# Forgetting heads' norms from whole squares, and the second four heads' keys turned by DMA

## The chip, the cores and the metric

The kernel runs on one core of one Trainium2 chip. The metric is the device time of one execution in microseconds (us); a lower time is better. PE is TensorE, ACT is ScalarE, DVE is VectorE, POOL is GpSimd and SP is SyncE, which issues most of the DMAs. PEld is the weight load of PE.

## The reference, cut to what matters

One layer on 256 tokens of width 2048: a combined projection, two groups of attention heads side by side, an output projection, and a feed-forward part. The change touches the queries and keys of the forgetting group, which has 8 heads of 128 columns:

```python
def rms_norm(x, g):
    x32 = x.astype(jnp.float32)
    y = x32 * lax.rsqrt(jnp.mean(x32 * x32, axis=-1, keepdims=True) + EPS)
    return (y * g.astype(jnp.float32)).astype(x.dtype)
...
    qa = rms_norm(to_heads(qa, N_HEADS_FOX), q_norm_l)
    ka = rms_norm(to_heads(ka, N_HEADS_FOX), k_norm_l)
    log_f = jax.nn.log_sigmoid((fa + b_forget_l).astype(jnp.float32))
    c = jnp.cumsum(log_f, axis=1).transpose(0, 2, 1)
    out_a = forgetting_attention(qa, ka, to_heads(va, N_HEADS_FOX), c)
```

So each head's row of 128 numbers is divided by the root of its mean square, and then queries and keys are needed with the head's columns on the partitions, which takes a transpose.

## The kernel before

All products are float32 split in two parts: ACT casts a weight block `w_raw` to its high part `w_hi` (line 277), DVE subtracts to get the low part `w_lo` (line 285), and PE multiplies with both. A *step* is one weight block. The code hands each step's instructions to the engines in a fixed order that is written out by hand (a schedule without a planner): in the loop at the end, at step n the cast and the subtraction of step n+2 are issued, the load of step n+6, and then the products of step n. Between groups of products `tick()` lets each unfinished piece of side work (a Python generator) run to its next `yield`. So one `yield` more or less moves all that follows in that piece by one tick, about one group of 12 matmuls on PE. Each engine works through its own list strictly in that order.

The projection is done in *units* of 11 steps. Unit A gives the queries and keys of forgetting heads 0 to 3 (tiles `rA00`, `rA01` for queries, tokens 0 to 127 and 128 to 255; `rA10`, `rA11` for keys), unit B those of heads 4 to 7 (`rB..`), unit C queries and keys of four stick-breaking heads (`rC..`), then a unit for values and unit D. Within a unit the products go to four PSUM banks in the order a, c, b, (e, b), a, (e, b), a, b, (c, a), a, (a, c); a pair in brackets is one step with two groups. Between them ACT (line 601) or DVE (line 607) takes a bank's contents out and the bank is then written on. The products of `oFox` and of the heads run beside the next units.

When a unit of the forgetting group is done, `fox_rows(half)` starts: squares and sums of squares of each head, the inverse root (`rsqrt`), the multiplication of the rows by it on DVE (line 710), then the transposes. For heads 0 to 3 the keys are turned by DMA: `send_heads` lets ACT put the two 16-bit halves of each word apart (line 646), SP issues a DMA transpose (line 650), and `take_heads` puts the halves together again (line 655). The queries, and before the change the keys of heads 4 to 7 too, are turned by PE against the identity (line 687, tile `ps_h`) and copied out by ACT (line 691). Then each head runs as `fox_head`: `ps_s` are its scores on PE, `qk` the split queries and keys, `pT` the turned weights, `ps_o` its output, which lands in `oFox`. Until a head lands, its part of `oFox` is not in use.

Of the kernel before, what the change touches and what calls it, by code (L numbers as in the profile page):

```python
# [12 lines left out]
AF = mybir.ActivationFunctionType  # L13
ALU = mybir.AluOpType
AX = mybir.AxisListType
# [4 lines left out]
NT = S // P  # L20
KT = D // P
HD = 128
# [25 lines left out]
def hybrid_layer(  # L48
# [20 lines left out]
    act, dve = nc.scalar, nc.vector  # L69
# [43 lines left out]
    gq = const.tile([P, 1], F32, name="gq")  # L113
# [20 lines left out]
    zeros = ccol.rearrange("p a b -> p (a b)")[:, :P]  # L134
# [32 lines left out]
    def rsqrt(out_, ss, scale, n, gap=2):  # L167
        a = small.tile([P, n], F32, name="rs_a", tag=f"rs_a{n}")
        y = small.tile([P, n], F32, name="rs_y", tag=f"rs_y{n}")
        u = small.tile([P, n], F32, name="rs_u", tag=f"rs_u{n}")  # L170
        dve.tensor_scalar(a, ss, scale, EPS, op0=ALU.mult, op1=ALU.add)
        for _ in range(gap):
            yield
        act.activation(y, a, AF.Ln)
        act.activation(y, y, AF.Exp, scale=-0.5)
        dve.tensor_tensor(u, a, y, op=ALU.mult)
        dve.tensor_tensor(u, u, y, op=ALU.mult)
        dve.tensor_scalar(u, u, -0.5, 1.5, op0=ALU.mult, op1=ALU.add)
        dve.tensor_tensor(out_, y, u, op=ALU.mult)
# [159 lines left out]
    oFox = late.tile([P, NH, S], F32, name="oFox")  # L339
# [11 lines left out]
    def heads_tile(name):  # L351
        return at.tile([P, 4, S], F32, name=name, tag="qk", bufs=2)
# [25 lines left out]
    tile_of = {}  # L378
# [264 lines left out]
    def send_turned(rows, room, moves=(act.copy, dve.tensor_copy)):  # L643
        planes = room.bitcast(U16).rearrange("p h s -> p (h s)").rearrange("p (t c) -> p t c", t=NT)
        for t, (move, (source, words)) in enumerate(zip(moves, rows)):
            move(
                planes[:, t].rearrange("p (b f) -> p b f", b=2),
                source.bitcast(U16).rearrange("p (f b) -> p b f", b=2),
            )
            nc.sync.dma_start_transpose(  # L650
                words.bitcast(U16).rearrange("p (g s) -> p g s", s=P), planes[:, t]
            )

    def take_turned(move, words, t, room):
        move(
            room.bitcast(U16).rearrange("p h (s b) -> p b h s", b=2)[:, :, :, t * P : (t + 1) * P],
            words.bitcast(U16).rearrange("p (b h s) -> p b h s", b=2, h=4),
        )

    def send_heads(rows, n, key, moves=(act.copy, dve.tensor_copy)):  # L660
        tile_of[key] = heads_tile(key)
        send_turned([(rows[n, t], rows[n, t]) for t in range(NT)], tile_of[key], moves)

    def take_heads(rows, n, key, moves):
        for t, move in enumerate(moves):
            take_turned(move, rows[n, t], t, tile_of[key])
# [13 lines left out]
    def to_heads(rows, which, keys, scales):  # L680
        for n, key, scale in zip(which, keys, scales):
            dst = tile_of[key] = heads_tile(key)
            pss = []
            for t in range(NT):
                ps = psb.tile([P, 4, P], F32, name="ps_h", tag="t")
                for h in range(4):
                    nc.tensor.transpose(ps[:, h, :], rows[n, t][:, h * HD : (h + 1) * HD], ident)
                pss.append(ps)
            yield
            for t in range(NT):  # L690
                act.activation(dst[:, :, t * P : (t + 1) * P], pss[t], AF.Identity, scale=scale)

    def fox_rows(half):
        def done(rows):
            order = [(1, 0), (1, 1), (0, 1), (0, 0)]
            ss = small.tile([P, 4, 4], F32, name="ss", tag="ss")
            rn = small.tile([P, 4, 4], F32, name="rn", tag="rn")
            for m, nt in enumerate(order):
                for h in range(4):
                    act.activation(  # L700
                        zeros, rows[nt][:, h * HD : (h + 1) * HD], AF.Square,
                        accum_out=ss[:, m, h : h + 1],
                    )
                if m < 3:
                    yield
            flat = "p a b -> p (a b)"
            yield from rsqrt(rn.rearrange(flat), ss.rearrange(flat), 1.0 / HD, 16)
            for m, nt in enumerate(order):
                r3 = rows[nt].rearrange("p (h d) -> p h d", h=4)
                dve.tensor_tensor(r3, r3, rn[:, m, :].unsqueeze(2).to_broadcast([P, 4, HD]), op=ALU.mult)  # L710
                if m % 2:
                    yield
                    if m == 1 and not half:
                        send_heads(rows, 1, "kA0", (act.copy, act.copy))
            while started["fox"] < 4 * half:
                yield
            if half:
                yield from to_heads(rows, (1, 0), ("kA1", "qA1"), (1.0, gq))
            else:
                yield  # L720
                yield from to_heads(rows, (0,), ("qA0",), (gq,))
                take_heads(rows, 1, "kA0", (act.copy, dve.tensor_copy))
            for h in range(4 * half, 4 * half + 4):
                waiting.append(fox_head(h, half))

        return done
# [808 lines left out]
```

## Time and profile before

| | us |
|---|---|
| median of 3 runs | 1088.14 (1087.89 to 1088.5) |
| the profiled execution's own time | 1089.65 |
| its span in the trace | 1087.9 |
| PE busy | 1082.6 |
| DVE busy | 929.5 |
| ACT busy | 776.1 |

The span is what the trace covers from the first instruction to the last. PE's busy time says that there is nearly always a matmul under way, and that is the first thing to hold against any change here: work taken off PE counts in full, and any new gap on PE counts in full as well. The page's other parts (waits, chain, stretches of the timeline) tell where PE was near a gap.

### The profile page before, as it was taken

The page shows a single profiled execution, that of the slowest core. Times are in us where ns is not written, and L with a number is a line of the kernel's source. Part 1 is how long each engine was busy: PE and PEld are TensorE (multiplying, and loading weights), DVE is VectorE, ACT ScalarE, POOL GpSimd, SP SyncE. Part 2 cuts the span into 40 slices and gives each one's busy share as a digit, 9 for nine tenths or more (in the row PEclk, how much of TensorE's full clock was granted, in tenths as well). Part 3 has the DMA queues.
Part 4 walks back from the last instruction along what each step waited for, and adds up shares of the span by engine and source line. Part 5 has one row for each costly group of instructions (what it writes and reads, how often), then busy time and mean ns, then how long its engine had stood idle before and what let it go on. Part 6 is the DMA issues. An engine that isn't in the chain of part 4 may idle for free.

```text
span 1087.9 us, 14614 instructions
## 1 busy us (share of the span) xinstructions
PE 1082.6 (100%) x5635; PEld 932.2 (86%) x5635; DVE 929.5 (85%) x928; ACT 776.1 (71%) x981; POOL 59.0 (5%) x53
## 2 busy tenths in 40 slices
PE   9999999999999999999999999999999999999998
PEld 9988888888878888888888888888888888888887
DVE  5988899898997877779888988889888898879896
ACT  6767798887876857667766767667767766667663
POOL 0000000001000000000000000000000010000000
PEclk9999999999999999999999999999999999999999
DMA  8897988999876666579899597987969698996995
GB/s 311 267 274 234 306 190 241 245 258 290 244 231 222 193 201 195 192 182 263 252 242 300 172 274 250 255 287 178 310 195 294 219 245 261 232 308 168 284 244 156
DMA packets 192688, 262.85 MB, mean 242 GB/s; under 512 B 22105, under 2 KB 115691, under 8 KB 192619
## 3 DMA queue, kind: packets, MB, share of 16 engines
q1 hardware_dynamic: 169162, 214.59, 59.5%
q0 software_dynamic: 23280, 47.19, 24.5%
q8 instruction: 44, 0.72, 0.3%
q14 instruction: 26, 0.20, 0.1%
q10 hardware_dynamic: 176, 0.14, 0.0%
HBM read 255.48 MB, written 2.10 MB: 237 GB/s over the span
## 4 chain that ended last, share of the span: by engine, by line
PE 89%; DVE 5%; issue 2%; DMA 2%; ACT 1%; DVEq 0%; ACTq 0%; POOLq 0%
PE pu L1268 41%; PE bank_a L305 16%; PE bank_b L305 10%; PE bank_c L305 6%; PE acc_o L305 5%; PE acc_v L425 4%; PE bank_e L305 3%; DVE w_lo L285 2%; DMA w_raw<-in_w_down_dram 2%; PE acc L305 2%; ACT w_hi L277 1%; PE ps_x L195 1%; PE ps_o L775 0%; DVE w_raw L996 0%; DVE xb L1290 0%
## 5 line engine op out<-in xcount | busy, mean ns | idle before, releaser
L285 DVE TENSOR_TENSOR w_lo<-w_raw,w_hi 128x2048 fp32r<-128x2048 f32 (+2 forms) x251 | 555.7, 2218 | 120.5 <-ACT w_hi L277 119.6
L277 ACT CAST w_hi<-w_raw 128x2048 fp32r<-128x2048 f32 (+2 forms) x251 | 464.4, 1853 | 205.1 <-PE pu L1268 84.4
L1268 PE MATMUL pu<-hT,w_hi 128*128 128x512 f32 x1408 | 333.5, 389 | 0.0
L1268 PEld LDWEIGHTS pu<-hT,w_hi 128*128 128x128 f32 x1408 | 262.9, 188 | 53.7
L1268 PEld LDWEIGHTS pu<-hT,w_lo 128*128 128x128 f32 x1408 | 180.0, 191 | 6.6
L1268 PE MATMUL pu<-hT,w_lo 128*128 128x256 f32 x1408 | 182.0, 283 | 0.0
L1321 POOL DMA_DIRECT2D w_raw<-in_w_down_dram x31 | 39.8, 1302 | 714.7 <-DVE w_lo L285 383.1
L1193 ACT ACTIVATE tap<-up,ccol 128x256 f32<-128x256 f32 x176 | 74.6, 495 | 0.0
L305 PE MATMUL bank_a<-w_hi,hT 128*128 128x512 f32 x192 | 48.6, 395 | 0.0
L305 PEld LDWEIGHTS bank_a<-w_hi,hT 128*128 128x128 f32 x192 | 35.2, 188 | 6.9
L305 PE MATMUL bank_b<-w_hi,s 128*128 128x512 f32 x160 | 40.1, 392 | 0.2 <-DVE xb L1290 0.2
L305 PE MATMUL bank_a<-w_hi,s 128*128 128x512 f32 x160 | 40.0, 392 | 0.0
L305 PE MATMUL bank_a<-w_hi,g 128*128 128x512 f32 x152 | 38.0, 392 | 0.0
L425 PE MATMUL acc_v<-w_hi,hT 128*128 128x344 f32 x192 | 36.1, 330 | 0.0
L305 PEld LDWEIGHTS bank_b<-w_hi,s 128*128 128x128 f32 x160 | 28.8, 189 | 5.8 <-issue 0.6
L305 PEld LDWEIGHTS bank_a<-w_hi,s 128*128 128x128 f32 x160 | 28.9, 189 | 5.2
L1186 ACT ACTIVATE gate<-up,ccol 128x256 f32<-128x256 f32 x44 | 24.1, 594 | 11.5 <-DVE up L1179 6.2
L1198 DVE TENSOR_TENSOR gate<-gate,tap 128x512 f32<-128x512 f32 x44 | 30.3, 688 | 2.3
L1198 DVE TENSOR_TENSOR val<-val,tap 128x512 f32<-128x512 f32 x44 | 30.3, 688 | 2.3
L305 PE MATMUL acc_o<-w_hi,oSb 128*128 128x512 f32 x128 | 31.7, 396 | 0.0
L1179 DVE TENSOR_TENSOR up<-t,R 128x512 f32<-128x512 f32 x44 | 30.5, 692 | 1.5
L305 PEld LDWEIGHTS bank_a<-w_hi,g 128*128 128x128 f32 x152 | 27.4, 189 | 5.0
(312 smaller groups left out, 1427.4 us busy)
## 6 DMA issues: line engine op xcount, KB each, us to landing
w_raw<-in_w_up_dram SPq DMA_DIRECT2D x88, 1024.0 KB, 6.8
w_raw<-in_w_down_dram SPq DMA_DIRECT2D x44, 1024.0 KB, 7.1
w_raw<-in_w_in_dram SPq DMA_DIRECT2D x40, 1024.0 KB, 6.8
w_raw<-in_w_down_dram POOLq DMA_DIRECT2D x31, 1024.0 KB, 9.9
w_raw<-in_w_out_dram SPq DMA_DIRECT2D x16, 1024.0 KB, 6.2
w_raw<-in_w_in_dram POOLq DMA_DIRECT2D x10, 1024.0 KB, 9.9
w_raw<-in_w_in_dram SPq DMA_DIRECT2D x13, 516.0 KB, 5.3
xb<-in_x_dram POOLq DMA_DIRECT2D x4, 512.0 KB, 9.3
```

The source lines that it names most:

```text
L195: nc.tensor.transpose(ps[:, j, t * P : (t + 1) * P], x2[:, t, (k + j) * P : (k + j + 1) * P], ident)
L277: copy(hi[:, :n], raw[:, :n])
L285: dve.tensor_tensor(lo[:, :n], raw[:, :n], f32(hi[:, :n]), op=ALU.subtract)
L305: nc.tensor.matmul(o, lhs(i, l, t), r[:, i, :] if cut is None else r[:, i, cut], start=starts and j == 0, stop=stops and j == 3 * n - 1, s ...
L425: nc.tensor.matmul(banks[j][t][:, :VC], of_half(hT[:, k], l, t), w[:, 0, m * VC : (m + 1) * VC], start=k == l == 0 and w is mem["parts", i ...
L1179: dve.tensor_tensor(u[:, :, 2:], t2, R, op=ALU.mult)
L1186: act.activation(a[:, j, :], u[:, j, 2:], AF.Identity, scale=ccol[:, 2, f : f + 1], bias=ccol[:, 3, f : f + 1],)
L1193: act.activation(taps[w][:, j, :], u[:, j, w : w + S], AF.Copy, scale=ccol[:, w, f : f + 1])
L1198: dve.tensor_tensor(a, a, tap, op=ALU.add)
L1268: nc.tensor.matmul(acc[:, j, S:] if low else acc[:, j, :], (lo if low else hi)[:, i, j * P : (j + 1) * P], hT[:, k, 0, :] if low else hT[: ...
L1321: nc.gpsimd.dma_start(mem[weights].rearrange("p (a b) -> p a b", a=4), plus, accum_op=ALU.add)
```

## The change

Three things change in `fox_rows`, for both halves unless said otherwise.

1. The 16 squares per half, each of one head's 128 columns with ACT's own sum (`accum_out`), become 4 squares of whole rows of 512 columns without a sum. They are written into `oFox`, and DVE sums the heads with 4 reductions to 4 values per row.
2. Two rows are squared per tick in place of one, so the piece has two `yield`s ahead of `rsqrt` and not three.
3. For heads 4 to 7 (`half` 1) the keys are no longer turned by PE but by DMA, as those of heads 0 to 3 are, with the upper half of `oFox` as the room for the 16-bit halves; ACT does all four of the copies around the two DMA transposes. `to_heads` then turns the queries alone.

```diff
-            for m, nt in enumerate(order):
-                for h in range(4):
-                    act.activation(
-                        zeros, rows[nt][:, h * HD : (h + 1) * HD], AF.Square,
-                        accum_out=ss[:, m, h : h + 1],
+            for first in (0, 2):
+                squared = [oFox[:, 2 * m : 2 * m + 2, :].rearrange("p a s -> p (a s)") for m in (first, first + 1)]
+                for m, rows_squared in enumerate(squared):
+                    act.activation(rows_squared, rows[order[first + m]], AF.Square)
+                yield
+                for m, rows_squared in enumerate(squared):
+                    dve.tensor_reduce(
+                        ss[:, first + m, :], rows_squared.rearrange("p (h d) -> p h d", h=4),
+                        axis=AX.X, op=ALU.add,
                     )
-                if m < 3:
-                    yield
...
-                    if m == 1 and not half:
-                        send_heads(rows, 1, "kA0", (act.copy, act.copy))
+                    if m == 1:
+                        if half:
+                            room = oFox[:, 4:8, :]
+                        else:
+                            room = tile_of["kA0"] = heads_tile("kA0")
+                        send_turned([(rows[1, t], rows[1, t]) for t in range(NT)], room, (act.copy, act.copy))
             while started["fox"] < 4 * half:
                 yield
             if half:
-                yield from to_heads(rows, (1, 0), ("kA1", "qA1"), (1.0, gq))
+                tile_of["kA1"] = heads_tile("kA1")
+                take_heads(rows, 1, "kA1", (act.copy, act.copy))
+                yield from to_heads(rows, (0,), ("qA1",), (gq,))
```

Lines behind the change stand a little lower in the new file: 710 becomes 712, and lines from 719 on move by 8 (the scores of a head from 798 to 806, for instance). The new squares are line 701, the new reductions line 704.

The change also moves instructions. Three places matter. The first is PE in unit C, from the score and output products around head 3 to the first transposes of unit B's rows. Before:

```order
L305 MATMUL bank_e_1463<-w_hi_1458,hT_95 128x512 x8
L305 MATMUL bank_e_1463<-w_lo_1459,hT_95 128x512 x4
L775 MATMUL ps_o_1576<-pT_1512,vA0_714 128x256 x2
L775 MATMUL ps_o_1576<-pT_1512,vA1_715 128x256
L798 MATMUL ps_s_1580<-cR_121,headR_92 128x384
L802 MATMUL ps_s_1580<-qk_1518 128x256 x3
L777 MATMUL ps_o_1576<-turned_1476,vA2_716 128x128
L804 MATMUL ps_s_1580<-kA0_1178,qA0_1216 128x128
L305 MATMUL bank_b_1432<-w_hi_1458,hT_95 128x512 x8
L305 MATMUL bank_b_1432<-w_lo_1459,hT_95 128x512 x4
L687 MATMUL ps_h_1615<-cs_84,rB10_1047 128x128 x4
L687 MATMUL ps_h_1620<-cs_84,rB11_1048 128x128 x4
```

The same place on PE now:

```order
L783 MATMUL ps_o_1541<-pT_1484,vA0_714 128x256 x2
L783 MATMUL ps_o_1541<-pT_1484,vA1_715 128x256
L806 MATMUL ps_s_1545<-cR_121,headR_92 128x384
L810 MATMUL ps_s_1545<-qk_1490 128x256 x3
L785 MATMUL ps_o_1541<-turned_1443,vA2_716 128x128
L812 MATMUL ps_s_1545<-kA0_1151,qA0_1189 128x128
L305 MATMUL bank_e_1470<-w_hi_1465,hT_95 128x512 x8
L305 MATMUL bank_e_1470<-w_lo_1466,hT_95 128x512 x4
L687 MATMUL ps_h_1594<-cs_84,rB00_1043 128x128 x4
L687 MATMUL ps_h_1599<-cs_84,rB01_1044 128x128 x4
L305 MATMUL bank_b_1430<-w_hi_1465,hT_95 128x512 x8
L305 MATMUL bank_b_1430<-w_lo_1466,hT_95 128x512 x4
```

The key transposes (`rB10`, `rB11`) are gone. The query transposes (`rB00`, `rB01`), which stood two groups further down (behind the group of bank a that follows this bank b), now stand between the groups e and b; and the products of head 3 stand one group earlier, ahead of e.

The second place is DVE in the same stretch of unit C, from the subtraction of step 4 on. Before:

```order
L285 TENSOR_TENSOR w_lo_1427<-w_raw_1164,w_hi_1426 128x2048
L819 RECIPROCAL rl_1449<-l_1445 128x2
L820 TENSOR_SCALAR pr_1446<-pr_1446,rl_1449 128x128
L821 TENSOR_SCALAR pr_1446<-pr_1446,rl_1449 128x256
L285 TENSOR_TENSOR w_lo_1459<-w_raw_1319,w_hi_1458 128x2048
L807 TENSOR_TENSOR ps_s_1477<-ps_s_1477,masksR_118 128x2x128
L809 TENSOR_REDUCE nm_1488<-ps_s_1477 128x1
L810 TENSOR_REDUCE nm_1488<-ps_s_1477 128x1
L171 TENSOR_SCALAR rs_a_1495<-ss_1389 128x16
```

The same place on DVE now, up to the subtraction of step 5:

```order
L827 RECIPROCAL rl_1416<-l_1412 128x2
L828 TENSOR_SCALAR pr_1413<-pr_1413,rl_1416 128x128
L829 TENSOR_SCALAR pr_1413<-pr_1413,rl_1416 128x256
L704 TENSOR_REDUCE ss_1386<-oFox_115 128x4 x2
L285 TENSOR_TENSOR w_lo_1425<-w_raw_1163,w_hi_1424 128x2048
L815 TENSOR_TENSOR ps_s_1444<-ps_s_1444,masksR_118 128x2x128
L817 TENSOR_REDUCE nm_1455<-ps_s_1444 128x1
L818 TENSOR_REDUCE nm_1455<-ps_s_1444 128x1
L704 TENSOR_REDUCE ss_1386<-oFox_115 128x4 x2
L171 TENSOR_SCALAR rs_a_1460<-ss_1386 128x16
L285 TENSOR_TENSOR w_lo_1466<-w_raw_1316,w_hi_1465 128x2048
```

Four reductions came in, and the head's work, `rs_a` and all that leads to the scaled rows stand one subtraction earlier than before. Between here and the scaling of the last row, `rB00`, there were the subtractions of steps 4 to 7; now there are those of steps 4 to 6.

The third place is ACT behind `rsqrt`'s logarithm and exponential, in unit C. Before:

```order
L174 ACTIVATE rs_y_1496<-rs_a_1495 128x16
L175 ACTIVATE rs_y_1496<-rs_y_1496 128x16
L601 ACTIVATE rC10_1397<-bank_a_1366,nrstd1_93 128x512
L277 CAST w_hi_1558<-w_raw_1290 128x2048
L860 ACTIVATE oFox_115<-ps_o_1576,pcol_86 128x256
L781 ACTIVATE ssq0_116<-ps_o_1576 128x256
L838 COPY turned_1515<-pr_1446 128x2x384
L851 CAST pT_1608<-turned_1515 128x256
L831 COPY turned_1611<-pr_1542 128x768
L277 CAST w_hi_1625<-w_raw_1430 128x2048
```

The same place on ACT now:

```order
L277 CAST w_hi_1523<-w_raw_1228 128x2048
L646 COPY oFox_115<-rB10_1045 128x1024
L646 COPY oFox_115<-rB11_1046 128x1024
L601 ACTIVATE rC10_1392<-bank_a_1368,nrstd1_93 128x512
L277 CAST w_hi_1563<-w_raw_1292 128x2048
L868 ACTIVATE oFox_115<-ps_o_1541,pcol_86 128x256
L789 ACTIVATE ssq0_116<-ps_o_1541 128x256
L846 COPY turned_1487<-pr_1413 128x2x384
L859 CAST pT_1584<-turned_1487 128x256
L839 COPY turned_1587<-pr_1508 128x768
L655 COPY kA1_1590<-rB10_1045 128x2x4x128
L655 COPY kA1_1590<-rB11_1046 128x2x4x128
```

The cast of step 8's weights (`w_hi_1625` before, `w_hi_1626` now), which stood directly behind line 831, now comes behind the two copies of line 655, head 3's two exponentials (lines 824 and 825) and the two evictions of the queries (line 691).

On SP the two new DMA transposes stand behind the load of unit C's last block and ahead of the load of the next unit's first.

## Prediction

> **What bounds the kernel now.** I read the page's parts 1 and 4 first, then PE's waits, then the chain, stretches and single rows around the two places where `fox_rows` runs.
>
> ```profile
> PE 1082.6 (100%) x5635; PEld 932.2 (86%) x5635; DVE 929.5 (85%) x928; ACT 776.1 (71%) x981; POOL 59.0 (5%) x53
> PE 89%; DVE 5%; issue 2%; DMA 2%; ACT 1%; DVEq 0%; ACTq 0%; POOLq 0%
> PEld acc_o L305 <- DVE xb L1104: 1.3, 3, 0.5
> PEld bank_b L305 <- ACT rB L601: 0.4, 1, 0.4
> ```
>
> PE bounds it: it is busy for 1082.6 of 1087.9 us, and its longest waits are near 1 us. So work off PE counts once, and a new gap counts once. The question is whether PE's operands still come in time where the change moves them, and the busy shares of the whole span don't tell that. The stretches do (us from the start; then length, busy us of PE, PEld, DVE, ACT, POOL):
>
> ```profile
> 98.00:114.00 16.00, 16.00 (x70) 12.83 (x70) 13.12 (x8) 15.13 (x41) 1.28 (x1) 1.00 0.92 222
> 139.00:157.00 18.00, 18.00 (x87) 15.03 (x86) 16.79 (x23) 17.62 (x51) 1.28 (x1) 1.00 0.84 197
> 157.00:172.00 15.00, 15.00 (x80) 12.67 (x79) 13.92 (x27) 14.81 (x26) 0.00 (x0) 1.00 0.99 282
> 172.00:188.00 16.00, 16.00 (x79) 13.55 (x78) 15.51 (x18) 13.90 (x22) 1.28 (x1) 1.00 0.75 216
> ```
>
> Around half 0 (first row) DVE has 2.9 us to spare in 16. Around half 1 (second and third) it has 2.3 in 33, and ACT 0.6. PE doesn't wait there all the same, because weights are split two steps ahead. This is PE's side of half 1, from the chain (start, length, what):
>
> ```profile
> 158.25 2.72 PE bank_e L305 x12
> 160.97 0.35 PE ps_o L775 x3
> 161.32 0.18 PE ps_s L798
> 161.50 0.35 PE ps_s L802 x3
> 161.85 0.22 PE ps_o L777 x2
> 162.07 0.22 PE ps_s L804 x2
> 162.29 2.76 PE bank_b L305 x12
> 165.05 0.87 PE ps_h L687 x8
> 165.93 2.81 PE bank_a L305 x12
> 168.73 0.87 PE ps_h L687 x8
> 169.61 2.79 PE bank_b L305 x12
> 172.40 0.36 PE ps_o L775 x3
> 172.76 0.22 PE ps_o L777 x2
> 172.98 2.74 PE bank_c L305 x12
> ```
>
> **What PE gains.** The key transposes at 165.05 go: 0.87 us. The wait of 0.4 us on ACT's line 601 stood behind a group of four squares; in half 0 ACT now reaches that eviction earlier, so I count half of it, 0.2 us. Together -1.1 us. These are the only terms on the path that must fall.
>
> **The squares on ACT and DVE.**
>
> ```profile
> L700 ACT ACTIVATE ccol<-rB x16: 302/312/324, 140.9 to 155.0; 128x128 f32<-128x128 f32 x16
> L700 ACT ACTIVATION_READ_ACCUMULATOR ccol<-rB x16: 185/187/207, 141.1 to 155.2; 128x1 f32 x16
> L213 ACT ACTIVATE spare<-xb x8: 616/632/635, 357.0 to 382.5; 128x512 f32<-128x512 f32 x8
> L810 DVE TENSOR_REDUCE nm<-ps_s 128x1 f32<-128x256 f32 x3 | 1.2, 413 | 0.0
> L809 DVE TENSOR_REDUCE nm<-ps_s 128x1 f32<-128x128 f32 x2 | 0.6, 292 | 0.1
> ```
>
> ACT loses 16 x (0.31 + 0.19 less some overlap, 0.43 from start to start) = 7 us per half and gets 4 x 0.63 = 2.5 us. This gain of 4.5 us is off PE's path. DVE gets 4 reductions over 512 columns. No row shows one; from 128 to 256 columns the reduction grows by 0.12 us, so 512 give 0.41 + 0.24 = 0.65 us, about 0.57 from start to start. Bounds are 0.41 (the row with 256) and 0.75 (line 607 on 512). That is 2.3 us more per half for DVE, the engine with 2.3 us to spare, between 1.6 and 3.0. In half 0 the spare 2.9 us and a tick's distance cover it.
>
> **The step that decides: the last row's scaling against PE's query transposes.** PE now wants `rB00` between the groups e and b: 160.97 (end of e) + 1.32 (head 3's five small groups, now ahead of e), less 0.1 to 0.2 for the earlier gain: 162.2. DVE's list ends with the scaling of `rB00`:
>
> ```profile
> 147.13 2.28 DVE L285 TENSOR_TENSOR w_lo<-w_raw,w_hi 128x2048 fp32r<-128x2048 f32 x1
> L285 DVE TENSOR_TENSOR w_lo<-w_raw,w_hi 128x2048 fp32r<-128x2048 f32 x5 | 11.4, 2285 | 1.9 <-ACT w_hi L277 1.9
> L793 DVE TENSOR_TENSOR qk<-kA,qk 128x256 fp32r<-128x256 f32 x2 | 0.8, 418 | 0.0
> 167.03 1.28 DVE L710 TENSOR_TENSOR rB<-rB,rn 128x512 f32<-128x512 f32 x2
> ```
>
> The second and third rows are of the stretch from 147.1 to 168.4. Before, from step 3's subtraction at 147.13 to the scaled `rB00` at 168.31 lie 21.2 us. Of them go: the idle 1.9 (DVE now has the reductions to do while the casts finish), one subtraction 2.2 (step 7's, now behind), and head 2's `qk` pair 0.55, which now stands ahead. The reductions add 2.3. That makes 18.9 us. Step 3's subtraction starts at about 147.2, as before: between the subtractions of steps 1 and 3 stand the same pieces, with head 2's `qk` pair in place of head 1's, which has moved ahead in turn. So `rB00` is ready at 166.1. PE waits 3.9 us for it. Once PE goes on, it is behind before's order by 166.1 - 162.3 = 3.8, and by 3.8 - 0.87 = 2.9 after the second set of transposes that it no longer has. With reductions at 0.41 this is 2.1; at 0.75, 3.4. Beforehand, at 158.1, head 3's `qk` and head 0's `pT` on DVE are late by some 0.4 us; that lies inside the same wait.
>
> **The wait behind it.** ACT's first copy of line 646 needs `rB10` scaled. Counted the same way this is done 5.0 us before `rB00` (`rB11` 0.6, step 6's subtraction 2.2, head 3's mask and maxima 1.0, two rows 1.2), at 161.1. ACT stood at this place at 159.9 before (162.32 below, less a cast and an eviction), and with fewer squares ahead it is now there at about 158. So ACT stands still for 3 us, and what is queued behind is: an eviction of bank a (needed by PE only two groups on), the cast for step 7, head 0's output, and then the two copies of line 655 ahead of the cast for step 8.
>
> ```profile
> L646 ACT COPY kA<-rA x2: 1043/1045/1047, 116.7 to 117.7; 128x1024 uint16<-128x1024 uint16 x2
> L655 ACT COPY kB<-rD x2: 1364/1368/1372, 298.7 to 299.9; 128x1024 uint16<-128x1024 uint16 x2
> 162.32 0.47 ACT L860 ACTIVATE oFox<-ps_o,pcol 128x256 f32<-128x256 f32 x1
> 165.10 1.91 ACT L277 CAST w_hi<-w_raw 128x2048 fp32r<-128x2048 f32 x1
> 174.28 0.74 DVE L607 SCALAR_TENSOR_TENSOR rC<-bank_a,nrstd,rC 128x512 f32<-128x512 f32 x1
> L650 SPq DMA_TRANSPOSE rA<-kA x2: 1607/2484/3361, 117.8 to 119.5; - x2
> rA<-kA SPq DMA_TRANSPOSE x2, 5.4
> rD<-kB SPq DMA_TRANSPOSE x2, 7.2
> ```
>
> From 161.1: two copies 2.0, the eviction 0.6, a cast 1.8, five pieces of heads 2.8 (162.32 to 165.10), two copies 2.7, head 3's exponentials 0.9, two evictions of queries 1.2, the cast of step 8 1.9: 175.0, where that cast ended at 167.0 before. The DMA transposes, issued near 162.3 and 164.0, land by 169.4 at 5.4 us, just before the second copy wants the second of them (169.6); at 7.2 they add 1.5 us. Then DVE: step 8's subtraction 2.2, an addition 0.7, head 4's `qk` 0.6, step 9's subtraction 2.2, the addition out of bank a (line 607, at 174.28 before) 0.7: 181.4. PE may write bank a, in the second group of step 8, only then. It gets there at 166.1 + 0.9 + 2.8 + 2.8 + 0.6 + 2.8 + 2.7 + 0.75 (head 4's scores, now ahead) = 179.4, and waits 2.0 us. Before it was there at 175.7 (172.98 + 2.74) without head 4's scores; 181.4 - 175.7 - 0.75 = **5.0 us** behind, savings included. Since ACT's list sets this time, a shorter first wait only makes this one longer. Behind it PE has given ACT and DVE 5 us, and I find no third wait: the load behind the new transposes on SP goes out when they have been issued (164.0 + 3.4, about 167) and is wanted two steps ahead of the next unit, after 180.
>
> **Against a rule.** DVE's reductions grow by 0.12 us for 128 columns, one column in 0.94 ns. The Trainium skill (VectorE: DVE Perf Modes, "Rules for kernel authors") expects tensor_reduce to run at 1x and calls it the slowest operation of the engine, and advises to restructure; it speaks against this change. By its rate alone the four would be about 0.53 us each (an estimate from that page's table), which would make the sum 4.7 in place of 5.0. The trace's two rows agree with the rate and add a fixed part, so the rows are used.
>
> **The rivals.**
> (a) *The cover holds* (the other side). If DVE had `rB00` scaled by 162.2, that is 3.9 us ahead of my count, and bank a out by 179, PE would keep the 1.1 us: 1087.0. For it: PE has no gap in the four stretches shown. Against it: 13.9 of 15 us busy on DVE and 14.8 on ACT. Chance 0.15.
> (b) *Only the first wait.* If ACT gets through its list 2 us faster (copies beside the landing, fewer heads' pieces in between), PE is behind by 2.9 alone: 1091.0. I put it with the forecast, as its lower part.
> (c) *The gap slows PE's clock.* At the start of the run, after PE's idle time, 8 passes of 128 columns took 2.08 us, 0.26 each, against 0.11 for the passes of line 804 above.
>
> ```profile
> 1.06 2.08 PE ps_i L189 x8
> ```
>
> If the 3.9 us gap put PE back into that pace for some 5 us, it would lose 2.7, of which the wait at bank a swallows 2.0: 1093.8. The Trainium skill (TensorE: Matmul & The Clock Gate, "What's actually happening") has the gate close after an idle window of about 3.4 us that runs free of the kernel; the gap is just longer, so a whole window seldom fits into it. No gap of this trace is long enough to tell. Chance 0.08.
> (d) *SP's queue.* The two transposes occupy SP for up to 5 us, and if the loads behind them came over 8 us late, steps of the next unit would starve: 1096 or more. Chance 0.06.
>
> **How the numbers follow.** The sum stands against the profiled span, 1087.9 + 5.0 = 1092.9; the median of the runs lies 0.24 above that span (the profiled execution's own time is 1089.65, which is not used), so 1093.1. The forecast with (b) has 0.68; its own range is 2.1 to 7 us more, 1090.0 to 1095.1. 0.03 is left for what I don't see. The range 1088.8 to 1096.0 leaves out (a) and part of (d). This kernel's measurement can tell about 0.2%, 2.2 us. Slower than 1090.3 are most of the forecast, (c) and (d): 0.76; within are (a) and the forecast's lower edge: 0.20; a gain over 2.2 us needs more than all that PE could save here: 0.04.
>
> **What would show it.** In the trace after: PE's weight load for `ps_h` waits for DVE's line 712 by 3 to 4 us near 162; ACT's line 646 on `oFox` waits about 3 us for line 712; a weight load into bank a waits about 2 us for line 607 near 179; the reductions of line 704 take near 0.65 us; nothing differs in the feed-forward part. I am wrong if PE shows no wait in unit C (then DVE kept up), if the reductions are far from 0.65, or if the time went elsewhere, such as to loads behind the new transposes.

## The result, and the profile after

The changed kernel takes 1096.87 us (median of 6 runs, 1096.66 to 1098.83); the kernel before takes 1088.32 beside it (6 runs). The ratio is 1.0081, interval 1.0071 to 1.0092: slower by 8.55 us, where 5.0 was forecast. 1096.87 lies just above the range given (1088.8 to 1096.0).

The page of the changed kernel, parts 1 and 4, and PE's weight-load waits (us in total, times, longest):

```profile
PE 1082.3 (99%) x5627; PEld 930.9 (85%) x5627; DVE 934.4 (85%) x936; ACT 770.9 (70%) x927; POOL 59.3 (5%) x53
PE 82%; DVE 7%; ACT 4%; issue 3%; DMA 3%; SPq 0%; DVEq 0%; ACTq 0%
PEld ps_h L687 <- ACT ssq L789: 3.9, 1, 3.9
PEld bank_b L305 <- ACT vB L601: 2.1, 1, 2.1
PEld bank_a L305 <- DVE rC L607: 1.4, 1, 1.4
PEld bank_a L305 <- DVE rB L607: 1.1, 1, 1.1
PEld ps_o L783 <- DVE ws L909: 0.9, 1, 0.9
```

PE is busy 0.3 us less and the span grew by 7.6: all of the loss is gaps. The first four of these waits were not there before, and the last was 0.5. A weight load begins to wait while PE still works on the group before, so PE's own gap is shorter (3.5 us in the first wait). In the first wait the name `ssq` is the page's guess: ACT's `ssq` ended at 166.94 and DVE's scaling of `rB00` at 166.89, too close to tell apart here. Other kernels tell: in keys_alone, tick_back and half0_later (below) PE starts `ps_h` 0.14 to 0.15 us behind that scaling, as here, while `ssq` ends 2.5 us ahead of PE's start in the first two and 4.1 us behind it in the third. So the scaling is what PE waits for. The stretches of before, read again, and the one behind them:

```profile
98.00:114.00 16.00, 16.00 (x71) 13.11 (x70) 15.80 (x17) 11.17 (x13) 1.28 (x1) 1.00 0.86 212
139.00:157.00 18.00, 18.00 (x88) 15.05 (x87) 17.83 (x26) 14.80 (x26) 2.18 (x2) 1.00 0.78 190
157.00:172.00 15.00, 11.31 (x58) 9.14 (x57) 12.22 (x21) 12.07 (x16) 0.00 (x0) 1.00 1.07 258
172.00:188.00 16.00, 14.81 (x73) 12.31 (x72) 13.41 (x19) 14.75 (x23) 0.00 (x0) 1.00 0.83 247
188.00:212.00 24.00, 22.27 (x110) 18.53 (x109) 22.66 (x29) 18.98 (x31) 2.57 (x2) 1.00 0.76 171
```

The columns are start and end, length, then busy us of PE, PEld, DVE, ACT and POOL, the granted clock of PE (1.00 is full speed), the DMA share and GB/s. Around half 0 DVE had 2.9 us to spare and now has 0.2; ACT has 4.0 and 2.8 us more to spare in the first two rows; PE has gaps in the last three rows: 3.7, 1.2 and 1.7 us.

Lateness means how much later than in the kernel before the same piece of work starts. Where it arises is read from PE's groups that stand in both kernels with the same heads' work ahead of them (start before, and how much later the same group starts after):

| place on PE | before | later by | new here |
|---|---|---|---|
| unit B, step 8 | 134.16 | 0.86 | 0.86, bank a waits for `rB` |
| unit C, behind the query transposes | 172.73 | 4.13 | 3.3, the wait at `ps_h` and one for `pT` (0.5) less the 0.87 saved |
| unit C, behind bank a | 182.24 | 5.61 | 1.5, the wait for `rC` |
| past the values unit's waits | 229.00 | 7.50 | 1.9, the wait at bank b |
| end of the stick-breaking heads | 323.87 | 8.24 | 0.7, in part the wait for `ws`; the rest was not followed |

From there on nothing is added but 0.3 at the very end. The profiled execution of before has two waits late in its feed-forward part:

```profile
PEld acc L305 <- DVE w_lo L285: 0.8, 1, 0.8
PEld bank_b L305 <- issue: 0.6, 1, 0.6
```

They are absent from the trace of after, whose lateness falls there from 8.24 to 7.29; without them the spans would differ by some 8.5, as the medians do (8.55).

### The profile page after: what moved, and what is told of

It is laid out like the page before. It is cut to its first block, busy times and chain, and to the rows that moved or that the text cites. A ratio compares the mean times of both kernels' runs of the same rounds, so it can differ in the third digit from the quotient of the medians.

```text
span 1095.5 us, 14556 instructions
## 1 busy us (share of the span) xinstructions
PE 1082.3 (99%) x5627; PEld 930.9 (85%) x5627; DVE 934.4 (85%) x936; ACT 770.9 (70%) x927; POOL 59.3 (5%) x53
## 4 chain that ended last, share of the span: by engine, by line
PE 82%; DVE 7%; ACT 4%; issue 3%; DMA 3%; SPq 0%; DVEq 0%; ACTq 0%
PE pu L1276 45%; PE bank_a L305 13%; PE bank_b L305 8%; PE acc_o L305 4%; PE acc_v L425 4%; PE bank_c L305 4%; DVE w_lo L285 4%; PE acc L305 2%; ACT w_hi L277 2%; PE bank_e L305 1%; DMA w_raw<-in_w_out_dram 1%; DMA pr<-turned 1%; DMA rA<-kA 0%; PE ps_x L195 0%; DVE ss L704 0%
## 5 line engine op out<-in xcount | busy, mean ns | idle before, releaser
L1276 PE MATMUL pu<-hT,w_lo 128*128 128x256 f32 x1408 | 182.0, 283 | 0.0
```

The source lines that it names most:

```text
L1276: nc.tensor.matmul(acc[:, j, S:] if low else acc[:, j, :], (lo if low else hi)[:, i, j * P : (j + 1) * P], hT[:, k, 0, :] if low else hT[: ...
```

## Experiments

All kernels ran beside the kernel before, whose median was 1088.2 to 1088.5 in each group. The theory is the prediction's, with sizes from the trace of after: operands are wanted before they can be there, and each such wait passes down ACT's and DVE's lists. The first four kernels take the change apart.

**norms_alone**: squares, reductions and the earlier `rsqrt` as in the change, keys turned by PE.

```diff
-                    if m == 1:
-                        if half:
-                            room = oFox[:, 4:8, :]
...
+                    if m == 1 and not half:
+                        send_heads(rows, 1, "kA0", (act.copy, act.copy))
...
+                yield from to_heads(rows, (1, 0), ("kA1", "qA1"), (1.0, gq))
```

> The new norms (whole squares, reductions on DVE, one tick earlier) with the keys of heads 4 to 7 turned by PE as before. Theory (lateness adds up along DVE and ACT): the 0.9 us that unit B lost stays, PE wants the scaled queries at about 165.9 and DVE has them at 166.9, so 1 us more; ACT has no new copies and catches up: before + 1.9, about 1090. Rival (the turned keys are harmless, the 2.4 us of reductions per half are the whole price): nearly all of the loss stays, 1095 to 1097. Rival (the transposes on SP and the copies are the whole price): as before, 1088.

Measured: 1091.61 us (1.0033, 1.0020 to 1.0045), with runs from 1089.77 to 1093.70. In the profiled execution, which took 1093.45, PE waits 2.8 us for `rB` in unit B, at most 0.6 at a time in unit C, and 1.4 for `vB` in the values unit. So in this execution unit B is worse than expected, and unit C better; the waits of the median run may be smaller.

**keys_alone**: before, with only the keys of heads 4 to 7 turned by DMA.

```diff
-                    if m == 1 and not half:
-                        send_heads(rows, 1, "kA0", (act.copy, act.copy))
+                    if m == 1:
+                        if half:
+                            room = oFox[:, 4:8, :]
...
+                take_heads(rows, 1, "kA1", (act.copy, act.copy))
+                yield from to_heads(rows, (0,), ("qA1",), (gq,))
```

> The keys of heads 4 to 7 turned by DMA, with the squares as before the change (16, with ACT's own sums, three ticks). Theory: PE still wants the queries one tick before it wanted them in the kernel before, at 165.1, and they are scaled at 168.3, so it waits 3 us; behind that ACT has 3.3 us more work and no gain from the squares: before + 5 to 6, 1093 to 1094.5. Rival (the reductions are the price): 1087.5 to 1088.5.

Measured: 1094.39 us (1.0057, 1.0045 to 1.0070), as expected. PE waits 3.8 us at `ps_h`. The cause of this wait is that `to_heads`, left with the queries alone, asks for them at the tick at which it asked for the keys, though they are scaled after the keys.

**tick_alone**: before, with two rows squared per tick.

```diff
-                if m < 3:
+                if m % 2:
                     yield
```

> The kernel before with two rows squared per tick in place of one, nothing else. Theory: rows and transposes move one tick ahead together, ACT has 7 us of squares in two ticks, unit B loses about 1 us and unit C nothing: 1089 to 1090. Rival (the shift of all that follows by a tick is the main price): 1093 or more. Rival (no effect): 1088.3.

Measured: 1094.70 us (1.0065, 1.0051 to 1.0079). This is far more than I expected, and the number of the rival (the shift of all that follows by a tick). The weight-load waits of its profiled execution, the shortest of five (1093.37):

```profile
PEld bank_b L305 <- ACT rB L601: 2.0, 1, 2.0
PEld bank_b L305 <- ACT rC L601: 1.5, 1, 1.5
PEld bank_a L305 <- DVE rB L607: 1.2, 1, 1.2
PEld ps_h L687 <- ACT pr L817: 0.9, 1, 0.9
```

With two rows per tick eight small squares and a cast stand together ahead of an eviction of line 601 (a bank's contents taken out), and bank b comes free late in both halves (first two lines); the third line is the wait of unit B, here without any reduction.

**tick_back**: the changed kernel with `rsqrt` at its old tick.

```diff
+            yield
             yield from rsqrt(rn.rearrange(flat), ss.rearrange(flat), 1.0 / HD, 16)
```

> The changed kernel with one more tick ahead of rsqrt, so that it comes at the tick it had before the change. Theory: unit B's 0.9 us go; in unit C the scaling and the query transposes both move one tick back, PE still waits 3 to 4 us for the scaled queries, and ACT and the values unit follow as now: about 1095. Rival (the shift by a tick is the main price): 1088 to 1090.

Measured: 1095.96 us (1.0071, 1.0059 to 1.0084). In the profiled execution, the longest of five (1097.63), the wait of unit B is gone and that at `ps_h` is 4.1.

**norms_three_ticks** came with a later group and completes the table: norms_alone with the same added `yield`.

> Whole squares and DVE's reductions alone, with rsqrt at the tick of before and the keys of heads 4 to 7 turned by PE as before. Theory (2.4 us more on DVE per half are covered when the rows aren't wanted earlier): 1087.8 to 1089.2. Rival (DVE has no cover for them): 1090 or more.

Measured: 1088.68 us (1.0003, 0.9994 to 1.0012): no difference. PE's longest wait outside the parts common to all is 0.5 us.

| squares | keys of heads 4 to 7 | ticks ahead of rsqrt | kernel | us |
|---|---|---|---|---|
| 16 with sums | PE | 3 | before | 1088.3 |
| 4 whole, DVE sums | PE | 3 | norms_three_ticks | 1088.68 |
| 4 whole, DVE sums | PE | 2 | norms_alone | 1091.61 |
| 16 with sums | PE | 2 | tick_alone | 1094.70 |
| 16 with sums | DMA | 3 | keys_alone | 1094.39 |
| 4 whole, DVE sums | DMA | 3 | tick_back | 1095.96 |
| 4 whole, DVE sums | DMA | 2 | after | 1096.87 |

With the keys on PE and three ticks, the reductions cost nothing that shows (1088.68). With the keys by DMA and three ticks the new norms come out 1.6 us slower (tick_back against keys_alone), but the runs overlap (1095.20 to 1097.63 against 1094.05 to 1096.17). With the keys on PE, two ticks cost 2.9 us with the new norms and 6.4 with the old squares, so ACT's 4.5 us per half seem to be worth something there; with the keys by DMA they cost 0.9. The keys by DMA cost 6.1 and 7.3 us with three ticks, and 5.3 with two. The losses don't add up: after has both and loses 8.6.

The next kernels move one demand at a time.

**half0_later**: the changed kernel, heads 0 to 3 asking one tick later.

```diff
             else:
                 yield
+                yield
                 yield from to_heads(rows, (0,), ("qA0",), (gq,))
```

> The changed kernel with one more tick ahead of the query transposes and the copies of line 655 of heads 0 to 3 alone. Theory: in unit B ACT and DVE no longer reach line 655 before the DMA transposes have landed, so the 0.9 us there go; unit C's loss stays, since the scaled queries of heads 4 to 7 are still wanted 4 us too early: 1095.5 to 1096. Rival (ACT's list alone sets where unit C ends up, so an earlier delay is swallowed): 1096.9 as now.

Measured: 1096.90 us (1.0081, 1.0068 to 1.0095). The wait of unit B is gone from its list and the time is as it was: the rival's number. PE is 0.5 us less late behind the values unit (7.0 at the row of 229.00); that doesn't show in the time.

**queries_two_later**: the changed kernel, heads 4 to 7 asking two ticks later.

```diff
             if half:
+                yield
+                yield
                 tile_of["kA1"] = heads_tile("kA1")
```

> The changed kernel with two more ticks ahead of the copies of line 655 and the query transposes of heads 4 to 7 alone, so that PE wants the scaled queries at about 169 in place of 162. Theory: the first wait goes and ACT's two copies no longer stand ahead of the cast of step 8, so the second wait and the one in the values unit go too; what is left is unit B's 0.9: 1088.5 to 1090. Rival (ACT's copies and the DMA transposes cost the time wherever they stand): 1093 or more.

Measured: 1093.39 us (1.0047, 1.0035 to 1.0060): 3.5 better than after, 4 worse than expected, and in the rival's range. The wait at `ps_h` is gone from its list, and the wait for `rC` at bank a is 2.8 us in place of 1.4. The two copies of line 655 now stand ahead of the cast of step 9 in place of step 8. So a shorter first wait makes the second one longer, as the prediction had it, but not by as much.

**takes_later**: the query transposes stay, the copies of line 655 go behind the cast of step 8.

```diff
-                tile_of["kA1"] = heads_tile("kA1")
-                take_heads(rows, 1, "kA1", (act.copy, act.copy))
                 yield from to_heads(rows, (0,), ("qA1",), (gq,))
+                tile_of["kA1"] = heads_tile("kA1")
+                yield
+                take_heads(rows, 1, "kA1", (act.copy, act.copy))
```

> The changed kernel with line 655's two copies for heads 4 to 7 behind the query evictions and a tick later, behind the cast of step 8. The query transposes stay where they are, so PE's first wait of 3.9 us stays. Theory (ACT's copies ahead of the cast of step 8 make the second wait): that cast ends near 172.7 in place of 175.2, the second wait of 1.4 us is gone or turns up one step later at most at 1 us: 1094.5 to 1096. Rival (all of unit C's loss is the first wait and what DVE does): 1096.9.

Measured: 1095.17 us (1.0068, 1.0054 to 1.0082). The wait of 3.9 at `ps_h` stays. The cast of step 8 ends at 173.1 and bank a is added at 180.3, in place of 175.2 and 181.6, so the copies ahead of that cast are part of what makes the second wait. Neither the second nor the third wait is in its list. But the clock was at half for 3.4 us behind the first wait here (the section on the hardware), which made PE later by itself, to 180.8 at bank a; without that some 1 us of the second wait would have stayed.

**head4_by_pe**: the changed kernel, head 4's weights turned by PE.

```diff
-        if 0 < h < NH - 1:
+        if 0 < h < NH - 1 and h != 4:
```

> The changed kernel with head 4's weights turned by PE in place of a DMA transpose, the one that took 9.4 us from issue to landing and for which ACT stood ahead of the eviction of line 601 in the values unit. Theory (that landing makes the third wait): the wait of 2.1 us shrinks to 1 or less, PE does 0.33 us more: 1095.3 to 1096.2. Rival (DVE and ACT are 7 us late there anyway, and PE inherits it): 1096.9 to 1097.5.

Measured: 1095.51 us (1.0065, 1.0053 to 1.0078), 1.4 less than after, and no wait of PE in the values unit: from 182.24 to 229.00 of the table above its lateness grows by 0.2 us, after's by 1.9. So head 4's DMA transpose makes the third wait.

**keys_alone_warm**: keys_alone, and PE kept busy during its gap.

```diff
                 ps = psb.tile([P, 4, P], F32, name="ps_h", tag="t")
+                if keys == ("qA1",) and t == 0:
+                    for h in range(24):
+                        nc.tensor.transpose(ps[:, h % 4, :], ident, ident)
```

> The kernel with the turned keys alone, and 24 transposes of the identity (2.6 us of PE work that nobody uses) ahead of the query transposes of heads 4 to 7, where PE otherwise stands idle for 3.1 us. Theory (the gap halves the granted clock for a window of 3.4 us and that costs 1.8 us of the 5.9): the clock stays at full and the time falls to 1092.3 to 1093. Rival (the later waits swallow it, so the slower clock costs nothing): 1094.4 as without them.

Measured: 1096.37 us (1.0073, 1.0059 to 1.0086), 2 us more than keys_alone; neither theory had that. The clock stayed at full behind the filled gap, but PE then waited 2.6 us for `rC` at bank a, a wait that keys_alone doesn't have, and the clock was halved behind that one. Against keys_alone its key rows were scaled 0.9 us later, before the added work; I can't say why. Its two runs at a mean clock of 1.0 took 1095.12 and 1095.21, still more than keys_alone. So it doesn't settle the clock's price in keys_alone; the section on the hardware has what the runs say of it.

The last kernels spread the ticks so that nothing is asked for early.

**spaced**: half0_later, with for heads 4 to 7 one more tick ahead of line 646, queries one tick later, and the copies of line 655 behind them. PE then runs in the order of before without the key transposes.

```diff
                         if half:
+                            yield
                             room = oFox[:, 4:8, :]
...
             if half:
+                yield
+                yield from to_heads(rows, (0,), ("qA1",), (gq,))
                 tile_of["kA1"] = heads_tile("kA1")
                 take_heads(rows, 1, "kA1", (act.copy, act.copy))
-                yield from to_heads(rows, (0,), ("qA1",), (gq,))
```

> Whole squares, reductions and turned keys as in the changed kernel, with the ticks spread anew: one more for heads 0 to 3 ahead of the query transposes; for heads 4 to 7 one more ahead of the copies of line 646, and the query transposes one later, with line 655's copies behind them. PE then has the query transposes where the kernel before had them. Theory (all the loss is early demand, and nothing of the change itself costs time): 1087 to 1088.8. Rival (2.4 us more on DVE per half can't be hidden in any order): 1090 or more.

Measured: 1090.12 us (1.0016, 1.0007 to 1.0025). 6.8 of the 8.6 us are gone; 1.8 stay.

**spaced_rows**: as spaced, with all four rows scaled ahead of line 646 and no tick between.

```diff
-                    if m == 1:
+                    if m == (3 if half else 1):
...
-                            yield
                             room = oFox[:, 4:8, :]
...
             if half:
                 yield
+                yield
                 yield from to_heads(rows, (0,), ("qA1",), (gq,))
```

> As the kernel with the ticks spread anew, but the rows of the queries are scaled one tick earlier: the one more tick for heads 4 to 7 stands no longer ahead of their scaling, and line 646's copies come behind the scaling of all four rows. Theory (what is left of the loss, 1.8 us, is the 1.5 us for which PE waits for the scaled queries): 1088 to 1089, the same as before within 0.1%. Rival (the lateness of DVE, which has 2.4 us more per half, comes out at another wait): 1090 as without it.

Measured: 1090.67 us (1.0021, 1.0012 to 1.0030). The 1.5 us at `ps_h` are gone; these came:

```profile
PEld bank_a L305 <- DVE rC L607: 1.1, 1, 1.1
PEld bank_e L305 <- DVE w_lo L285: 0.9, 1, 0.9
PEld bank_a L305 <- DVE vB L607: 0.7, 1, 0.7
```

**spaced_act_sums**: as spaced_rows, heads 4 to 7 with the 16 old squares, two rows per tick, and no reductions.

```diff
+            for m, nt in enumerate(order if half else ()):
+                for h in range(4):
+                    act.activation(
+                        zeros, rows[nt][:, h * HD : (h + 1) * HD], AF.Square,
+                        accum_out=ss[:, m, h : h + 1],
+                    )
+                if m % 2:
+                    yield
-            for first in (0, 2):
+            for first in (() if half else (0, 2)):
```

> The kernel with spread ticks and rows scaled early, but for heads 4 to 7 the sums are ACT's again (16 squares with accum_out, two rows per tick), so DVE has 2.4 us less and ACT 4.5 us more there. Theory (what remains is ACT's list, with copies that the keys on PE didn't need): slower than with DVE's sums, 1092 to 1094. Rival (what remains is DVE's 2.4 us): 1088 to 1089.5.

Measured: 1090.67 us (1.0023, 1.0014 to 1.0032), the same. Its list has a wait of 1.3 us for `rC` at bank b, now for ACT's line 601, and then the same 0.9 and 0.7. So without the reductions of heads 4 to 7 nothing is won back; but ACT has 4.5 us more there and makes a wait of its own, so this doesn't show that DVE's 2.4 us have no part in what stays.

**spaced_takes**: as spaced_rows, the two copies of line 655 a tick apart.

```diff
-                take_heads(rows, 1, "kA1", (act.copy, act.copy))
+                take_turned(act.copy, rows[1, 0], 0, tile_of["kA1"])
+                yield
+                take_turned(act.copy, rows[1, 1], 1, tile_of["kA1"])
```

> The kernel with spread ticks and rows scaled early, with the second copy of line 655 for heads 4 to 7 one tick behind the first, so that the cast of step 9 stands behind one copy and not two. Theory (what remains is ACT's copies ahead of a cast): that cast ends 1.2 us earlier and the wait at bank a, 1.1 us, goes: 1089.3 to 1090. Rival (DVE's list, or the loss has moved on to the values unit): 1090.7 as without it, or more.

Measured: 1092.38 us (1.0043, 1.0030 to 1.0055), worse: heads 4 to 7 start a tick later, and new waits stand further down (1.4 at `ps_z`, 1.3 for `pT`). The wait of 1.1 at bank a stayed.

Against norms_three_ticks the turned keys thus cost 1.4 to 2.0 us even in spaced and spaced_rows, though they take 0.87 us off PE. ACT's squares in place of the reductions don't win it back (spaced_act_sums); whether it is ACT's copies, the transfers, DVE's reductions beside them, or the spread of the ticks itself is open. No kernel here beats the one before.

## Why the prediction was right in direction and short in size

**The deciding step: right.** DVE had `rB00` at 166.1 by the count and at 166.9 in the trace. The count itself, 18.9 us from step 3's subtraction to `rB00`, is what the trace has; but that subtraction started at 148.0 and not at 147.2, since DVE came late out of unit B. PE came late to its place as well, at 163.5 where 162.2 was counted. The two latenesses largely cancel, so that the wait of 3.9 (3.5 as PE's own gap) hits the forecast of 3.9 in part by luck. Behind it, the chain of waits in unit C (start, length, what):

```profile
161.20 0.70 DVE rB L712
161.90 0.02 issue
161.92 2.00 ACT oFox L646 x2
163.92 0.58 ACT rC L601
164.50 1.79 ACT w_hi L277
...
169.07 2.47 ACT kA L655 x2
171.54 0.31 ACT pr L824 x2
171.85 0.45 ACT pr L825 x2
172.30 1.15 ACT qA L691 x2
173.46 1.79 ACT w_hi L277
...
180.88 0.74 DVE rC L607
```

It is the chain that was written down, link by link: `rB10` at 161.9 (161.1 forecast), the cast of step 8 done at 175.2 (175.0), bank a added at 181.6 (181.4). ACT stood still ahead of it, as forecast at 3:

```profile
ACT oFox L646 <- DVE rB L712: 2.9, 1, 2.9
L704 DVE TENSOR_REDUCE ss<-oFox x8: 673/676/680, 105.3 to 155.8; 128x4 f32<-128x512 f32 x8
```

The reductions took 0.676 us each against 0.65. Unit C adds 4.8 us to PE's lateness (from 0.9 to 5.6); the forecast was 5.2, from 0.2 early to 5.0 late. PE waits at bank a 1.4 and not 2.0, because it got there 1.1 us later than counted (180.5 against 179.4) and the bank came free only 0.2 later.

**"In half 0 the spare 2.9 us and a tick's distance cover it": wrong.** The spare time covers the reductions (norms_three_ticks). The tick's distance is just what is lacking: the tick taken away also brings line 655 forward by one step. In the kernel before, ACT came to line 655 only behind the cast that leads to the addition out of bank a (cast at 120.93, DVE's subtraction at 123.46, addition at 125.66); now line 655 stands ahead of that cast, which is at 123.68 in the chain below. I had gone through the tick for heads 4 to 7 only. The chain in unit B:

```profile
117.27 5.11 DMA rA<-kA
122.38 0.03 ACTq L655
...
123.68 1.91 ACT w_hi L277
...
127.83 0.76 DVE rB L607
128.59 0.04 issue
128.63 3.06 PE bank_a L305 x12
```

ACT waits 1.2 us for the landing of the first keys' DMA transposes (1.0 before, without a wait of PE behind it), its next cast is late, DVE's addition out of bank a behind that, and PE is 0.86 us late where -0.2 was booked. half0_later removes the wait, though not the time. In norms_alone's profiled execution the landing comes later, ACT stands 2.9 us for it, and the same wait of PE is 2.8 us.

**"I find no third wait": wrong, 1.9 us, and 0.7 behind it.** I ended the walk at bank a and argued that PE had by then given ACT and DVE 5 us. But PE's lateness came from theirs: at 182 PE is 5.6 late, and the subtraction that started at 174.94 before starts at 182.21, 7.3 late. The loads behind them, whose buffers that subtraction frees, go out as late. One of them now stands right ahead of head 4's transpose on SP:

```profile
195.40 9.37 DMA pr<-turned
204.77 0.02 issue
...
204.85 1.08 ACT turned L846
...
207.59 0.59 ACT vB L601
208.19 0.04 issue
208.23 3.01 PE bank_b L305 x12
```

ACT stands for the landing 1.2 us, and line 601's eviction behind it frees bank b late. head4_by_pe takes this out, with 1.4 us of time. The place of the copy behind the landing counts too: in takes_later that transpose lands 8.4 us after its issue, heads 4 to 7 stand a tick later, and PE doesn't wait. It is near rival (d): a transfer and a load in SP's order, but with the load ahead of a head's transpose, where I had looked only at the load behind the new transposes.

**The rivals.** (a) didn't occur; its condition, operands in time, is met in norms_three_ticks. (b) gave 2.9 for the first wait alone; 3.3 were measured, the small wait for `pT` included. (c) did not occur in the profiled execution; the row of 157 to 172 above has the clock at 1.00 through a gap of 3.5 us. It may have occurred in other runs: four of the six have a mean clock of 0.998, and 3.4 us at half speed in 1095 take 0.0016 off the mean. These four took 1096.76 to 1098.83 us, the other two (0.999) 1096.66 and 1097.24, so no price is plain. The rule of the Trainium skill that was weighed (VectorE: DVE Perf Modes, "Rules for kernel authors") put a reduction at 0.53 us by its 1x rate; the trace has 0.676, and its advice against them isn't borne out where the keys stay on PE, since there they cost nothing that shows (norms_three_ticks).

**The sum.** Behind bank a PE is 5.6 us late where 5.0 was forecast. Not in the sum were 1.9 in the values unit, 0.7 behind it and 0.3 at the very end. With the 0.6 they are the 3.5 us between 5.0 and 8.55, and the values unit, put at nothing by "I find no third wait", is the largest of them. The 0.9 in unit B is part of the 5.6, and no price of it shows: half0_later is without that wait and takes the same time.

## What to carry to other kernels

When work is dropped from a piece whose steps are spread over ticks, ask of every remaining step whether it has moved forward against the transfer or the scaling that feeds it; here the tick cost 0.9 to 6.4 us and the dropped key transposes 5.3 to 7.3, while the reductions, with the keys on PE, cost nothing that shows. A step moved off the bounding engine saves its time once (0.87 us), while copies ahead of a cast, on an engine that is 98% busy in that stretch, can cost more. Follow the lateness of the helping engines, not that of the bounding one, until they have caught up.

## What the runs showed of the hardware

**A DMA transpose lands behind the load that was issued ahead of it on SP.** The load and head 4's transpose in four kernels, each answer for the short stretch in which the two were issued (last column: us from issue to landing), after, then before, queries_two_later and spaced_rows:

```profile
w_raw<-in_w_in_dram SPq DMA_DIRECT2D x1, 1024.0 KB, 9.2
pr<-turned SPq DMA_TRANSPOSE x1, 9.4
```

```profile
w_raw<-in_w_in_dram SPq DMA_DIRECT2D x1, 1024.0 KB, 9.5
pr<-turned SPq DMA_TRANSPOSE x1, 3.1
```

```profile
w_raw<-in_w_in_dram SPq DMA_DIRECT2D x1, 1024.0 KB, 9.1
pr<-turned SPq DMA_TRANSPOSE x1, 3.7
```

```profile
w_raw<-in_w_in_dram SPq DMA_DIRECT2D x1, 1024.0 KB, 9.5
pr<-turned SPq DMA_TRANSPOSE x1, 5.3
```

The transpose was issued 0.5, 7.2, 6.1 and 4.9 us behind the load, and landed 0.7 to 0.8 us behind the load's landing each time. In all fourteen traces that show both landings it landed 0.5 to 0.8 us behind it, though its issue stood 0.5 to 7.2 us behind the load's. The time of this transpose from issue to landing, 3 to 10 us, is thus read from the load ahead of it, not from a median. Whether its data or only its signal was held up, these answers don't tell. The Trainium skill (DMA: Bandwidth & Descriptors, "Queues, rings and completion order") states that a transfer's signal of completion lands only after every earlier write of the same DMA engine, across its queues. The fourteen traces agree with that; that another queue wouldn't help, as it implies, wasn't tried.

**The clock was halved behind gaps of PE, for 3.4 us at a time.** Two stretches of keys_alone, most of the gap and what follows, and two of after (columns as above):

```profile
165.00:168.10 3.10, 0.02 (x1) 0.05 (x1) 3.06 (x7) 3.00 (x6) 0.00 (x0) 1.00 1.13 307
168.10:171.50 3.40, 3.40 (x13) 2.94 (x14) 0.17 (x1) 3.40 (x3) 0.00 (x0) 0.56 0.61 107
```

```profile
162.00:166.50 4.50, 1.55 (x7) 0.94 (x5) 4.47 (x7) 4.50 (x5) 0.00 (x0) 1.00 1.12 331
166.50:170.00 3.50, 2.96 (x17) 2.63 (x18) 2.93 (x3) 3.47 (x6) 0.00 (x0) 1.00 1.02 278
```

In keys_alone PE stood still for 3.4 us (164.65 to 168.08). Behind that the clock was at half for 3.41 us, so that eight transposes and the group behind them took 5.3 us from start to start, against 3.7 before: 1.6 us. Behind the gap of after's profiled execution (3.5 us) it stayed at full; behind the same gap in takes_later it was halved. Shorter gaps were enough elsewhere, at bank a in keys_alone_warm (first row) and in queries_two_later (second row; PE's gap in brackets):

```profile
181.07 3.29 PE L305 MATMUL bank_a<-w_hi,hT 128*128 128x512 f32 x8 [2.22 <-DVE rC L607]
178.56 2.54 PE L305 MATMUL bank_a<-w_hi,hT 128*128 128x512 f32 x8 [2.34 <-DVE rC L607]
```

Behind these the clock was at 0.50 from 182.0 to 184.8 and from 180.4 to 183.2. The Trainium skill (TensorE: Matmul & The Clock Gate, "What's actually happening") gives a free-running window of about 3.4 us, which agrees with the length of the stretch at half clock; that the gate closes only after an idle window doesn't, since gaps of 2.2 and 2.3 us were enough here.

What it costs in time is not settled. Of keys_alone's five runs the one with a mean clock of 1.0 took 1094.25 us, three with 0.998 took 1094.05 to 1094.40, and one with 0.996 took 1096.17. In queries_two_later two runs at 1.0 took 1093.35 and 1093.54, three at 0.998 took 1093.19 to 1094.26. In keys_alone_warm two runs at 1.0 took 1095.12 and 1095.21, three at 0.998 took 1096.37 to 1098.26. So in the first two kernels one such stretch shows no price, and in the third it may show one of a us or more.
